# Carrying the later keys' sum through one row of the triangular operand, and rounding the attention weights on another engine

## The chip, the core and the metric

The kernel runs on one core of a Trainium2 chip. The metric is the device time of one execution in microseconds. A core has a matrix engine (TensorE, PE in the profile; its weight loads are PEld), a vector engine (VectorE, DVE), an engine for activation functions (ScalarE, ACT), a general engine (GpSimd, POOL) and one that only issues transfers (SyncE, SP). Each works through its own instructions in order; semaphores between them keep the order of the data. SBUF is the on-chip memory with 128 partitions, PSUM the smaller one that TensorE writes its sums to, here in banks of 128 x 512 fp32.

## What is computed

One layer of a decoder with 512 tokens and 1024 channels: a mixer of two branches (causal stick-breaking attention with 8 heads of 64, and a short gated convolution), a cross-attention into 256 memory tokens, a SwiGLU feed-forward part and a final norm. The change lies in the stick-breaking attention alone:

```python
z = jnp.einsum('bhqd,bhkd->bhqk', qb, kb) * scale
mask = k_pos < q_pos
log_fail = jnp.where(mask, jax.nn.log_sigmoid(-z), 0.0)
log_later = lax.cumsum(log_fail, axis=3, reverse=True) - log_fail
weights = jnp.where(mask, jnp.exp(jax.nn.log_sigmoid(z) + log_later), 0.0)
outs.append(jnp.einsum('bhqk,bhkd->bhqd', weights, vb))
```

With e = softplus(z), which is -log_sigmoid(-z), the weight of query t on key s is exp(z - sum of e over all keys from s up to t - 1). So each key needs the sum of `e` over itself and over all later keys.

## The kernel before

Scores are held transposed: keys on the partitions, queries along the columns. The heads are taken in four pairs `p`, and within a pair the key tiles of 128 from the last to the first, `kt` = 3, 2, 1, 0. Key tile `kt` sees the queries from its own first token on, so n = 512 - 128 kt columns for each head. For kt = 3 and 2 both heads of a pair share one PSUM bank (256 and 512 columns), for kt = 1 and 0 each head has its own (384 and 512); `heads_of` says which. This makes 16 steps, listed in `steps`.

All products are made in a rounded fp32 form (`F32R`) from a high and a low half: ScalarE casts the high half, VectorE subtracts it from the value to get the low half.

A step has three parts, each written by one function.

- `scores(p, kt)` (L399): TensorE makes z (L408). ScalarE makes |z|, exp(-|z|) and ln(1 + .) (L415 to L417), VectorE e = max(z, 0) + that (L418), GpSimd masks it (`causal`, L376), and `lsplit` (L388) makes the halves `l` (L390 on ScalarE, L391 on VectorE). For kt = 2 and 1 the running sum of all later tiles is then added to `e` (L430, VectorE), and that sum is split once more into the halves `r` (`rest`, L390 and L391). For kt = 3 the sum is `e` itself, so `l` serves.
- `weights(p, kt)` (L440): onto z in its bank TensorE adds, for kt < 3, minus the later tiles' sum (L448: `neg1`, all -1, by the two halves in `rest`) and then minus the sum within the tile (L451: `negtri`, the triangle of -1, by the two halves of `l`). ScalarE takes the exponential (L453) into `a`, GpSimd masks it, VectorE multiplies it by the token's norm factor `r0` and rounds it to `ah` (L457), and makes the low half `al` (L458).
- `values(p, kt)` (L463): TensorE multiplies both halves by the values (L470) into a bank that is summed over the key tiles. After kt = 0 the two parts of a head are joined (L478, L479).

The steps are spread over projections that have nothing to do with them (`project`: 24 matmuls of 512 columns, L154 to L156; their weights are loaded by SyncE, cast by ScalarE in L149 and split by VectorE in L150; `wpool` holds four of each, and their results leave their two PSUM banks through VectorE). In step i the loop writes the scores of step i + 1 into the middle of that step's projections, then the weights of step i, then the values of step i - 1. A planner, not the program, sets each engine's final order from these and its own estimates. The score banks are a ring of four (`pz`): a bank is free for new scores when its exponential is read. The tiles of `l` and `r` come from `lpool` and hold one step each of their kind.

Of the kernel before, what the change touches and what calls it, by code (L numbers as in the profile page):

```python
# [8 lines left out]
F32 = mybir.dt.float32  # L9
F32R = mybir.dt.float32r  # L10
AF = mybir.ActivationFunctionType
ALU = mybir.AluOpType

P = 128
# [3 lines left out]
TT = S // P  # L18
# [25 lines left out]
def hybrid_layer(ctx: ExitStack, tc: tile.TileContext, xT_d, memT_d, cols_d, wv_d, win_d,  # L44
# [18 lines left out]
    def nm(s):  # L63
        count[0] += 1
        return f"{s}{count[0]}"
# [7 lines left out]
    def f(ap):  # L73
        return ap.bitcast(F32)
# [19 lines left out]
                            pattern=[[-1, P]], channel_multiplier=1)  # L94
    negtri = cpool.tile([P, P], F32R, tag="negtri", name="negtri")
    nc.vector.tensor_copy(negtri, tri_f)
    eps_t = cpool.tile([P, 1], F32, tag="eps_t", name="eps_t")
    nc.vector.memset(eps_t, EPS)
    nc.vector.memset(neg_f, 1.0 / D)
# [271 lines left out]
    def span(kt):  # L371
        return kt * P, S - kt * P
# [6 lines left out]
    def heads_of(kt):  # L379

        return ((0, 1),) if kt >= TT - 2 else ((0,), (1,))

    def by_head(t, n):
        return t.rearrange("p (h c) -> p h c", c=n)

    rest, later = {}, {}

    def lsplit(t, n, tag, bufs):  # L388
        hi, lo = (lpool.tile([P, n], F32R, tag=tag, name=nm(tag), bufs=bufs) for _ in range(2))
        nc.scalar.copy(hi, t)  # L390
        nc.vector.tensor_tensor(out=lo, in0=t, in1=f(hi), op=ALU.subtract)  # L391
        return hi, lo

    def part_of(parts, hs, some, n):

        i = hs.index(some[0])
        return [t[:, i * n:(i + len(some)) * n] for t in parts]

    def scores(p, kt):  # L399
        c0, n = span(kt)  # L400
        keys = slice(kt * P, (kt + 1) * P)
        zs[p, kt] = []
        for hs in heads_of(kt):
            bank = ztile("z")
            zs[p, kt].append(bank)
            for i, h in enumerate(hs):
                for part in range(2):
                    nc.tensor.matmul(bank[:, i * n:(i + 1) * n], ks[p][h][:, keys],  # L408
                                     qs[p][h][part][:, c0:], start=i + part == 0, stop=part == 1,
                                     skip_group_check=True)  # L410
        for hs, bank in zip(heads_of(kt), zs[p, kt]):
            w = len(hs) * n
            z = bank[:, :w]
            e = tmp("e")[:, :w]
            nc.scalar.activation(e, z, AF.Abs)  # L415
            nc.scalar.activation(e, e, AF.Exp, scale=-1.0)
            nc.scalar.activation(e, e, AF.Ln, bias=1.0)  # L417
            nc.vector.scalar_tensor_tensor(out=e, in0=z, scalar=0.0, in1=e, op0=ALU.max,  # L418
                                           op1=ALU.add)
            causal(by_head(e, n))  # L420
            bufs = 4 // len(hs)
            sp[p, kt, hs] = lsplit(e, w, f"l{kt}", bufs)
            if kt == TT - 1:
                later[hs] = e
                rest[p, kt - 1, hs] = sp[p, kt, hs]
            elif kt > 0:
                t = by_head(e, n)[:, :, P:]
                before = heads_of(kt + 1)[0] if len(heads_of(kt + 1)) == 1 else hs
                old = by_head(part_of([later[before]], before, hs, n - P)[0], n - P)
                nc.vector.tensor_tensor(out=t, in0=t, in1=old, op=ALU.add)  # L430
                later[hs] = e
                rest[p, kt - 1, hs] = lsplit(e, w, f"r{kt}", bufs)

    def carried(p, kt, hs):

        n = span(kt + 1)[1]
        before = hs if (p, kt, hs) in rest else (0, 1)
        return [by_head(t, n) for t in part_of(rest[p, kt, before], before, hs, n)]

    def weights(p, kt):  # L440
        c0, n = span(kt)
        av[p, kt] = {}
        for hs, bank in zip(heads_of(kt), zs[p, kt]):
            w = len(hs) * n
            z = bank[:, :w]
            if kt < TT - 1:
                for part in carried(p, kt, hs):
                    nc.tensor.matmul(by_head(z, n)[:, :, P:], neg1, part, start=False, stop=False,  # L448
                                     skip_group_check=True)
            for part in sp[p, kt, hs]:  # L450
                nc.tensor.matmul(z, negtri, part, start=False, stop=True, skip_group_check=True)  # L451
            a = tmp("a")[:, :w]
            exps.append(nc.scalar.activation(a, z, AF.Exp))  # L453
            causal(by_head(a, n))
            ah, al = unit("ah")[:, :w], unit("al")[:, :w]
            r = r0[:, kt:kt + 1]
            nc.vector.tensor_scalar(out=ah, in0=a, scalar1=r, scalar2=None, op0=ALU.mult)  # L457
            nc.vector.scalar_tensor_tensor(out=al, in0=a, scalar=r, in1=f(ah), op0=ALU.mult,  # L458
                                           op1=ALU.subtract)
            for h in hs:  # L460
                av[p, kt][h] = part_of((ah, al), hs, (h,), n)
# [902 lines left out]
```

## Time and profile before

| what | us |
|---|---|
| median of 3 runs | 851.78 |
| lowest and highest | 851.10, 851.84 |
| the profiled execution | 850.78 |
| its span, first to last instruction | 849.1 |
| TensorE busy | 838.4 (99%) |
| VectorE busy | 656.2 (77%) |
| ScalarE busy | 458.4 (54%) |
| GpSimd busy | 159.7 (19%) |

The attention lies from about 44 to 196 us of the span. TensorE's clock was granted in full (0.998). A row of a group reads: line, engine, operation, output and inputs by the program's names, shape, count, then busy time in us and the mean of one in ns, then the engine's idle time just before them and what ended it. A row of the timeline reads: start, duration, engine, line, operation. A row of the chain of work that ended last has the start, the time that the piece held the chain, and the line with its count. A row of the waits says who waited for whom, then the total in us, how often, and the longest. "(+2 forms)" means that the group mixes several widths.

### The profile page before, as it was taken

To read this page: it belongs to the slowest core of one execution; us is meant where nothing else is said; L and a number is where in the kernel's file an instruction comes from. 1 tells how busy PE (TensorE), PEld (TensorE's weight loads), DVE (VectorE), ACT (ScalarE), POOL (GpSimd) and SP (SyncE) were. 2 spreads that over 40 slices of the span, in tenths; PEclk is the share of its full clock that TensorE was granted. 3 is DMA by queue.
4 is the path that set the end of the run, shared out by engine and by line. 5 is a ranking of instruction groups with operands and counts; after the bars stand their busy time and mean duration, and the time that the engine had idled before them with its cause. 6 is when DMAs were issued, how large, how long until landed. Compare 5 with 4: busy or idle time off the path is not lost.

```text
span 849.1 us, 12662 instructions
## 1 busy us (share of the span) xinstructions
PE 838.4 (99%) x4778; PEld 737.8 (87%) x4778; DVE 656.2 (77%) x1043; ACT 458.4 (54%) x810; POOL 159.7 (19%) x171
## 2 busy tenths in 40 slices
PE   9999999999999999999999999999999999999996
PEld 7888887888888899888888789999999999888885
DVE  7869989896766586587455679888887888999786
ACT  7567767474333344444444556655555555576664
POOL 0013221120566640163000101111111110000001
PEclk9999999999999999999999999999999999999999
DMA  8542232225588765566431335767767772465552
GB/s 298 156 142 64 93 117 75 75 76 183 200 310 309 297 245 190 174 230 247 151 81 49 112 75 142 181 174 187 186 176 187 190 186 85 155 221 196 171 187 99
DMA packets 50510, 141.62 MB, mean 167 GB/s; under 512 B 5521, under 2 KB 7569, under 8 KB 47634
## 3 DMA queue, kind: packets, MB, share of 16 engines
q1 hardware_dynamic: 40818, 105.93, 36.7%
q0 software_dynamic: 9344, 34.62, 15.7%
q8 instruction: 37, 0.61, 0.3%
q10 hardware_dynamic: 288, 0.28, 0.1%
q14 instruction: 23, 0.19, 0.1%
HBM read 125.07 MB, written 13.64 MB: 163 GB/s over the span
## 4 chain that ended last, share of the span: by engine, by line
PE 95%; DVE 3%; ACT 1%; issue 0%; DMA 0%; POOL 0%; SPq 0%; ACTq 0%
PE z L817 15%; PE p L1083 11%; PE y L817 7%; PE pr L154 7%; PE pr L155 7%; PE pr L156 7%; PE v L817 4%; PE r L156 3%; PE r L154 3%; PE r L155 3%; PE v L272 3%; PE mq L156 2%; PE mq L154 2%; PE br L155 2%; PE br L154 2%; PE mq L155 2%
## 5 line engine op out<-in xcount | busy, mean ns | idle before, releaser
L149 ACT CAST wh<-wr 128x1024 fp32r<-128x1024 f32 x84 | 88.0, 1052 | 151.7 <-issue 70.9
L150 DVE TENSOR_TENSOR wl<-wr,wh 128x1024 fp32r<-128x1024 f32 x84 | 110.6, 1318 | 37.0 <-ACT wh L149 36.9
L154 PE MATMUL pr<-xgh,wh 128*128 128x512 f32 x288 | 112.7, 391 | 0.0
L155 PE MATMUL pr<-xgl,wh 128*128 128x512 f32 x288 | 112.3, 390 | 0.0
L156 PE MATMUL pr<-xgh,wl 128*128 128x512 f32 x288 | 112.3, 390 | 0.0
L552 POOL TENSOR_TENSOR pre<-pre 128x512 f32<-128x512 f32 x44 | 72.1, 1642 | 31.4 <-DMA pre<-in_w_ffn_out_dram 29.1
L786 POOL DMA_DIRECT2D ws<-in_w_ffn_in_dram x22 | 26.5, 1207 | 258.4 <-DVE wf L807 104.7
L817 PE MATMUL z<-xdh,wf 128*128 128x256 f32 x352 | 70.5, 283 | 0.2 <-ACT sb L838 0.2
L156 PEld LDWEIGHTS pr<-xgh,wl 128*128 128x128 f32 x288 | 54.1, 188 | 11.5
L154 PEld LDWEIGHTS pr<-xgh,wh 128*128 128x128 f32 x288 | 54.1, 188 | 10.6
L155 PEld LDWEIGHTS pr<-xgl,wh 128*128 128x128 f32 x288 | 54.1, 188 | 10.3
L838 ACT COPY sa<-z 128x256 f32<-128x256 f32 x44 | 16.4, 373 | 79.2 <-PE z L817 79.1
L817 PEld LDWEIGHTS z<-xdh,wf 128*128 128x128 f32 x352 | 57.3, 189 | 0.5 <-ACT sb L838 0.4
L807 DVE TENSOR_TENSOR wf<-s,wf 128x512 fp32r<-128x512 f32 x44 | 30.3, 691 | 26.0 <-ACT wf L806 25.8
L817 PE MATMUL z<-xdl,wf 128*128 128x256 f32 x176 | 49.8, 283 | 0.0
L898 DVE TENSOR_TENSOR wl<-wr,wh 128x1024 fp32r<-128x1024 f32 x33 | 40.3, 1220 | 4.4 <-ACT wh L965 4.2
L965 ACT CAST wh<-wr 128x1024 fp32r<-128x1024 f32 x33 | 34.6, 1049 | 7.0 <-DMA wr<-sums 3.3
L817 PE MATMUL z<-xch,wf 128*128 128x256 f32 x176 | 35.4, 284 | 0.1
L817 PE MATMUL v<-xoh,wf 128*128 128x256 f32 x176 | 35.4, 283 | 0.0
L817 PE MATMUL y<-xch,wf 128*128 128x256 f32 x176 | 35.4, 283 | 0.0
L817 PE MATMUL z<-xf,wf 128*128 128x256 f32 x264 | 35.4, 283 | 0.0
L817 PE MATMUL y<-xoh,wf 128*128 128x256 f32 x176 | 35.3, 283 | 0.0
(337 smaller groups left out, 2403.3 us busy)
## 6 DMA issues: line engine op xcount, KB each, us to landing
wr<-in_w_in_dram SPq DMA_DIRECT2D x36, 512.0 KB, 3.3
pre<-in_w_ffn_out_dram POOLq DMA_DIRECT2D x11, 1024.0 KB, 8.0
sums<-pre POOLq DMA_DIRECT2D x11, 1024.0 KB, 5.0
ws<-in_w_ffn_in_dram SPq DMA_DIRECT2D x22, 512.0 KB, 3.7
wg<-in_w_ffn_in_dram SPq DMA_DIRECT2D x22, 512.0 KB, 4.0
ws<-in_w_ffn_in_dram POOLq DMA_DIRECT2D x22, 512.0 KB, 6.4
wr<-sums SPq DMA_DIRECT2D x22, 512.0 KB, 3.9
wr<-in_w_ffn_out_dram SPq DMA_DIRECT2D x16, 512.0 KB, 3.5
```

Of the source, the lines that this page charges most:

```text
L149: after(nc.scalar.copy(h2, raw), lead[-1:])
L150: lows.append(nc.vector.tensor_tensor(out=l2, in0=raw, in1=f(h2), op=ALU.subtract))
L154: nc.tensor.matmul(ps, a[0], b[0], start=start, stop=False, **kw)
L155: nc.tensor.matmul(ps, a[0], b[1], start=False, stop=False, **kw)
L156: nc.tensor.matmul(ps, a[1], b[0], start=False, stop=stop, **kw)
L552: nc.gpsimd.tensor_tensor(out=t[:, a, :], in0=t[:, a, :], in1=t[:, b, :], op=ALU.add)
L786: nc.gpsimd.dma_start(s13, a[:, 0:4:3, :], accum_op=ALU.add)
L807: nc.vector.tensor_tensor(out=w[:, 1, :], in0=raw, in1=f(w[:, 0, :]), op=ALU.subtract)
L817: nc.tensor.matmul(ps[:, :HS], a, b, start=i < 3 and k == 0 and j == 0, stop=k == KP - 1 and j == 2, skip_group_check=True)
L898: nc.vector.tensor_tensor(out=lo, in0=src, in1=f(hi), op=ALU.subtract)
L965: nc.scalar.copy(hi, raw)
L1083: nc.tensor.matmul(res[i][s2], a[:, ts], b, start=j == 0 and n == 0, stop=n == 2 and j == (BEHIND - 1 if (i, s2) == (5, 1) else NJ - 1))
```

## The change

The later tiles' sum no longer has matmuls of its own. It is written into the first key's row (partition 0) of the triangular operand `l` of the next tile: `negrow` is `negtri` with -1 in all of its first row, so whatever stands in the operand's row 0 is subtracted for every key of the tile. The first key's own `e`, which stood there, only concerns its own row of the result, and VectorE subtracts it from the bank's row 0 directly. `lsplit` puts both halves into one tile, and GpSimd clears row 0 for the tile's own first 128 queries, which see no later tile.

The sum itself is read off the bank: after the triangular matmul, row 0 of the bank holds the first key's z minus all `e` of this and of all later tiles. ScalarE keeps a copy of the raw row 0 (`before`, taken in `scores`), and in `weights` the new function `carry` subtracts the one from the other on VectorE, ScalarE casts the high half into row 0 of the next tile's operand, and VectorE makes the low half there. So the running sum in `e`, its second split and the `neg1` matmuls are gone, and each tile's triangular matmul now depends on the one before it.

Apart from that, `ah` is made by ScalarE (a copy with the scale `r0`) instead of VectorE.

```diff
+    negrow = lpool.tile([P, P], F32R, tag="negrow", name="negrow", bufs=1)
+    nc.vector.tensor_copy(negrow, tri_f)
+    nc.vector.tensor_copy(negrow[0:1, :], neg_f[0:1, :])
...
-    rest, later = {}, {}
-
-    def lsplit(t, n, tag, bufs):
-        hi, lo = (lpool.tile([P, n], F32R, tag=tag, name=nm(tag), bufs=bufs) for _ in range(2))
+    before = {}
+
+    def lsplit(t, n, heads, kt):
+
+        w = heads * n
+        both = lpool.tile([P, 2, w], F32R, tag=f"l{kt}", name=nm("l"), bufs=2 // heads)
+        hi, lo = both[:, 0, :], both[:, 1, :]
         nc.scalar.copy(hi, t)
         nc.vector.tensor_tensor(out=lo, in0=t, in1=f(hi), op=ALU.subtract)
+        if kt < TT - 1:
+            row = f(both)[0:1].rearrange("o a (h c) -> o a h c", c=n)
+            nc.gpsimd.memset(row[:, :, :, :P], 0.0)
         return hi, lo
...
             nc.scalar.activation(e, z, AF.Abs)
+            if kt > 0:
+                row = before[p, kt, hs] = lpool.tile([1, w], F32, tag="s", name=nm("s"), bufs=3,
+                                                     padded_shape=[1, 512])
+                nc.scalar.copy(row, z[0:1])
             nc.scalar.activation(e, e, AF.Exp, scale=-1.0)
...
             causal(by_head(e, n))
-            bufs = 4 // len(hs)
-            sp[p, kt, hs] = lsplit(e, w, f"l{kt}", bufs)
-            if kt == TT - 1:
-                later[hs] = e
-                rest[p, kt - 1, hs] = sp[p, kt, hs]
-            elif kt > 0:
-                t = by_head(e, n)[:, :, P:]
-                before = heads_of(kt + 1)[0] if len(heads_of(kt + 1)) == 1 else hs
-                old = by_head(part_of([later[before]], before, hs, n - P)[0], n - P)
-                nc.vector.tensor_tensor(out=t, in0=t, in1=old, op=ALU.add)
-                later[hs] = e
-                rest[p, kt - 1, hs] = lsplit(e, w, f"r{kt}", bufs)
...
+            if kt < TT - 1:
+                nc.vector.tensor_tensor(out=z[0:1], in0=z[0:1], in1=e[0:1], op=ALU.subtract)
+            sp[p, kt, hs] = lsplit(e, n, len(hs), kt)
+
+    def carry(p, kt, hs, z, n):
+
+
+        row = lpool.tile([1, len(hs) * n], F32, tag="c", name=nm("c"), bufs=2,
+                         padded_shape=[1, 512])
+        nc.vector.tensor_tensor(out=row, in0=before.pop((p, kt, hs)), in1=z[0:1], op=ALU.subtract)
+        for some in heads_of(kt - 1):
+            if hs[0] not in some and some[0] not in hs:
+                continue
+            src, = part_of([row], hs, some, n)
+            hi, lo = (by_head(t[0:1], n + P)[:, :, P:] for t in sp[p, kt - 1, some])
+            src = by_head(src, n)
+            nc.scalar.copy(hi, src)
+            nc.vector.tensor_tensor(out=lo, in0=src, in1=f(hi), op=ALU.subtract)
...
-            if kt < TT - 1:
-                for part in carried(p, kt, hs):
-                    nc.tensor.matmul(by_head(z, n)[:, :, P:], neg1, part, start=False, stop=False,
-                                     skip_group_check=True)
+            tri = negtri if kt == TT - 1 else negrow
             for part in sp[p, kt, hs]:
-                nc.tensor.matmul(z, negtri, part, start=False, stop=True, skip_group_check=True)
+                nc.tensor.matmul(z, tri, part, start=False, stop=True, skip_group_check=True)
             a = tmp("a")[:, :w]
             exps.append(nc.scalar.activation(a, z, AF.Exp))
+            if kt > 0:
+                carry(p, kt, hs, z, n)
             causal(by_head(a, n))
             ah, al = unit("ah")[:, :w], unit("al")[:, :w]
             r = r0[:, kt:kt + 1]
-            nc.vector.tensor_scalar(out=ah, in0=a, scalar1=r, scalar2=None, op0=ALU.mult)
+            nc.scalar.activation(ah, a, AF.Copy, scale=r)
```

More of the change, by code (lines that the diff above doesn't have):

```diff
@@ L420, in scores @@
             causal(by_head(e, n))
-            bufs = 4 // len(hs)
-            sp[p, kt, hs] = lsplit(e, w, f"l{kt}", bufs)
-            if kt == TT - 1:
-                later[hs] = e
-                rest[p, kt - 1, hs] = sp[p, kt, hs]
-            elif kt > 0:
-                t = by_head(e, n)[:, :, P:]
-                before = heads_of(kt + 1)[0] if len(heads_of(kt + 1)) == 1 else hs
-                old = by_head(part_of([later[before]], before, hs, n - P)[0], n - P)
-                nc.vector.tensor_tensor(out=t, in0=t, in1=old, op=ALU.add)
-                later[hs] = e
-                rest[p, kt - 1, hs] = lsplit(e, w, f"r{kt}", bufs)
[L434 to L438, printed above, removed]
+            if kt < TT - 1:
[13 more added lines that the diff above has]
+            nc.vector.tensor_tensor(out=lo, in0=src, in1=f(hi), op=ALU.subtract)
     def weights(p, kt):
```

## The prediction, made before the changed kernel was run

> **What bounds the kernel now.** I read the chain of work that ended last first, then the busy times of the stage that the change touches, then that stage's waits.
>
> ```profile
> PE 95%; DVE 3%; ACT 1%; issue 0%; DMA 0%; POOL 0%; SPq 0%; ACTq 0%
> 44.00:196.00 152.00, 151.04 (x720) 126.83 (x719) 130.81 (x213) 103.87 (x189) 35.37 (x60) 1.00 0.30 97
> ```
>
> The second row is the stage of the stick-breaking attention, from the first score matmul to the last value matmul. After the bounds and the length (152.00 us) come the busy times of PE, its weight loads, VectorE (DVE), ScalarE (ACT) and GpSimd (POOL). TensorE is without work for 0.96 us of it, so time leaves this stage only if TensorE gets less to do, and is lost wherever another engine makes it wait. VectorE stands at 130.81 of 152 (86%), ScalarE at 103.87 (68%): the first has little room, the second some.
>
> **Part 1: the matmuls that go.** The carry `neg1` x `rest` (L448) is no longer multiplied.
>
> ```profile
> L448 PE MATMUL z<-r,neg 128*128 128x384 f32 x16 | 4.1, 337 | 0.0
> L448 PE MATMUL z<-r,neg 128*128 128x256 f32 x16 | 3.2, 281 | 0.0
> L448 PE MATMUL z<-l,neg 128*128 128x256 f32 x8 | 1.6, 282 | 0.0
> 93.60 0.24 PE z L448 x2
> 114.13 0.35 PE z L448 x2
> ```
>
> The first three rows group them: 40 instructions, 24 with 256 columns and 16 with 384. Their mean durations include the pipeline, so the price is the pace in the chain: 0.24 us for a pair of 256 columns, 0.35 for a pair of 384. 12 x 0.24 + 8 x 0.35 = **5.7 us** that TensorE no longer streams. The stage's lower end for TensorE is 152.0 - 5.7 = 146.3 us. The triangular matmuls stay as many and as wide; `negrow` takes the place of `negtri` as their weights.
>
> **Part 2: VectorE.** In each of the four head pairs the changed groups are: kt=3 one of 256 columns, kt=2 one of 512, kt=1 two of 384, kt=0 two of 512.
>
> ```profile
> L430 DVE TENSOR_TENSOR e<-e,e 128x256 f32<-128x256 f32 x12 | 5.7, 486 | 0.0
> L391 DVE TENSOR_TENSOR r<-e,r 128x384 fp32r<-128x384 f32 (+1 forms) x12 | 7.4, 617 | 0.8 <-ACT r L390 0.8
> L457 DVE TENSOR_SCALAR ah<-a,r 128x512 fp32r<-128x512 f32 (+2 forms) x24 | 11.1, 464 | 3.8 <-POOL a L376 3.8
> L418 DVE SCALAR_TENSOR_TENSOR e<-z,e 128x512 f32<-128x512 f32 x12 | 8.0, 684 | 1.8 <-ACT e L417 1.8
> L391 DVE TENSOR_TENSOR l<-e,l 128x384 fp32r<-128x384 f32 x8 | 4.4, 554 | 0.8 <-ACT l L390 0.8
> L391 DVE TENSOR_TENSOR l<-e,l 128x256 fp32r<-128x256 f32 x4 | 1.7, 424 | 2.0 <-ACT l L390 2.0
> L313 DVE TENSOR_TENSOR k<-qk,k 64x512 fp32r<-64x512 f32 x8 | 5.5, 686 | 0.3
> ```
>
> The first three rows go: 5.7 + 7.4 + 11.1 = 24.2 us. What comes works on one partition. The last row shows that 64 partitions cost what 128 do (686 against 684 ns for 512 columns), so I price one partition like 128. No row shows one partition on VectorE, nor VectorE writing the score bank in PSUM: it could be nearly free, or dearer by about as much as the difference between the rows above. New are the subtraction of `e`'s row from the bank (12 of 512, 8 of 384 columns), the difference row (4 of 512, 8 of 384, 4 of 256) and the low half of the carry (8 of 384, 12 of 256): 16 x 0.684 + 16 x 0.554 + 4 x 0.424 + 8 x 0.554 + 12 x 0.424 = 31.0 us. **Net +6.8 us**: VectorE comes to 137.6 us against 146.3 us for TensorE, 94%.
>
> [...]
>
> **Part 3: ScalarE.**
>
> ```profile
> L390 ACT CAST l<-e 128x512 fp32r<-128x512 f32 x12 | 7.5, 621 | 11.5 <-POOL e L376 11.5
> L390 ACT CAST l<-e 128x384 fp32r<-128x384 f32 x8 | 4.0, 517 | 1.6 <-POOL e L376 1.6
> L390 ACT CAST l<-e 128x256 fp32r<-128x256 f32 x4 | 1.6, 406 | 8.8 <-POOL e L376 8.8
> L390 ACT CAST r<-e 128x384 fp32r<-128x384 f32 (+1 forms) x12 | 6.5, 548 | 5.9 <-DVE e L430 5.8
> L176 ACT ACTIVATE vmh<-vm,rm 128x512 fp32r<-128x512 f32 x4 | 2.7, 690 | 1.9 <-PE vm L156 1.9
> L201 ACT COPY vrow<-varb 1x512 f32<-1x512 f32 x1 | 0.6, 576 | 1.8 <-PE varb L190 1.8
> ```
>
> The `r` casts go (6.5 us). The last row is a copy of one partition out of PSUM: 576 ns, so one partition is hardly cheaper here. Coming: the score rows (4 of 512, 8 of 384, 4 of 256: 8.2 us), the high halves of the carry (8 of 384, 12 of 256: 9.0), and `ah` with its scale, 0.07 us dearer than a cast by the `vmh` row (12 x 0.69 + 8 x 0.59 + 4 x 0.48 = 14.9). **Net +25.6 us**: 129.5 us, 88% of 146.3.
>
> **Part 4: GpSimd, the start, the memory.** 20 memsets of a row are new.
>
> ```profile
> 4.46 0.43 DVE L241 CAST wvh<-wk 128x512 fp32r<-128x512 f32 x1 [2.08 <-DMA wk<-in_w_value_dram]
> L347 POOL MEMSET cu<- x4: 100/102/104, 0.9 to 108.2; 128x2 f32 x4
> 0.79 0.20 POOL masks.py:197 MEMSET ident<- 128x128 f32 x1 [0.29 <-POOLq L1354]
> 99.08 1.61 POOL L498 TENSOR_TENSOR accm<-accm,mk 128x256 f32<-128x256 f32 x2
> 99.14 0.95 DVE L457 TENSOR_SCALAR ah<-a,r 128x512 fp32r<-128x512 f32 x1 [0.30 <-POOL a L376]
> ```
>
> From 0.10 us for 2 elements and 0.20 for 128 I estimate 0.3 us for 256 and 0.5 for 512 (16 and 4 of them): 6.8 us on an engine that is busy for 35 of 152. They cost time only where the triangular matmul waits for one (0.3 us, used below). The 99.08 and 99.14 rows show an `ah` stretched to 0.95 us beside a GpSimd add, against 0.46 on the mean of its kind: half of the time beside it. At that rate the memsets would stretch VectorE by 3.4 us. I take 0, since a memset reads nothing, and keep 3.4 for the range.
>
> [...]
>
> Two casts of 128 columns for `negrow` stand at the start, where VectorE waits 2.08 us for the first weights anyway (first row): nothing. The loads and their queues are not touched.
>
> **Part 5: where TensorE now waits.** Two places, both behind VectorE's queue.
>
> ```profile
> 102.49 1.22 DVE L150 TENSOR_TENSOR wl<-wr,wh 128x1024 fp32r<-128x1024 f32 x1
> 109.86 1.22 DVE L150 TENSOR_TENSOR wl<-wr,wh 128x1024 fp32r<-128x1024 f32 x1
> 110.78 0.56 PE L408 MATMUL z<-q,k 128*128 128x128 f32 x4
> 112.38 0.68 DVE L391 TENSOR_TENSOR l<-e,l 128x512 fp32r<-128x512 f32 x1
> 115.29 0.46 PE z L451 x2
> 149.51 0.68 DVE L391 TENSOR_TENSOR l<-e,l 128x512 fp32r<-128x512 f32 x1
> 153.23 0.46 PE z L451 x2
> 187.00 0.69 DVE L391 TENSOR_TENSOR l<-e,l 128x512 fp32r<-128x512 f32 x1 [0.47 <-ACT l L390]
> 189.43 0.46 PE z L451 x2
> ```
>
> First, a score bank is now free only when VectorE has read its row, not when ScalarE's exponential is done. The scores at 110.78 need the bank of kt=1. TensorE comes there 0.72 us sooner (three pairs of 0.24), at 110.06. If the row read stands behind the `wl` of 109.86, it ends at 111.08 + 0.55 = 111.6: a wait of 1.5 us, with the next projection queued behind it. If it stands ahead: 0. I take the middle, 0.75, at the three such places (pair to pair): 2.3 us.
>
> Second, the triangular matmul of kt=0 is where a pair has most of its new VectorE work ahead of it: between the kt=2 and the kt=0 matmuls 6.2 us come (two subtractions each at kt=1 and kt=0, rows for kt=2 and kt=1, four low halves) and 2.7 go (two `e` sums, two `r` halves, one `ah`), net 3.5. Three `wl` of 1.22 us stand there (first and last quoted), each for a projection three ahead (`wpool` holds four), so they can slide; if two do, 3.5 - 2.4 + 0.3 for the memset = 1.4 us is added. Today's margins from the end of the last `l` to its matmul are 2.2, 3.0 and 1.7 us in the pairs 1 to 3 (I take none for pair 0); TensorE comes 1.42 us sooner (three pairs of 0.24, two of 0.35). That leaves waits of 0.6, 0 and 1.1 us. The first is already paid by the 0.75 ahead of it; the last stands. Sum of both: 2.3 + 1.1 = **3.4 us**.
>
> **The sum.** -5.7 + 3.4 = -2.3 us. The profiled execution took 850.78 us (span 849.1 and 1.7 around it), 1.0 below the median of the runs, 851.78. Against the median: **849.5 us**. The ends of the unknowns: no new wait, 846.1; with 1.5 at all three places and no `wl` slid (3.8 added, waits of 3.0, 2.2 and 3.5 at kt=0), 10.2 us of waits, 856.3.
>
> **The rivals.** *Full gain.* The planner orders VectorE so that the row reads and carries go first; TensorE waits nowhere: 846.1 us. For it stands this row of the windows:
>
> ```profile
> 100.00:111.00 11.00, 11.00 (x56) 9.38 (x54) 10.89 (x17) 7.44 (x13) 2.15 (x5) 1.00 0.31 98
> ```
>
> From 100 to 111 us VectorE is busy for 10.89 of 11.00 us today and TensorE still doesn't wait. Against it: three engines at 88% or more.
>
> *VectorE becomes the bound.*
>
> ```profile
> DVE e L418 <- ACT e L417: 5.1, 3, 3.0
> DVE ah L457 <- POOL a L376: 3.8, 7, 1.7
> DVE l L391 <- ACT l L390: 3.3, 6, 1.0
> ACT l L390 <- POOL e L376: 21.8, 13, 4.2
> ACT r L390 <- DVE e L430: 5.8, 5, 1.9
> ```
>
> If VectorE's own waits of 12.2 us (first three rows) stay as they are, `al` waiting for ScalarE instead of `ah` for GpSimd, it needs 137.6 + 12.2 = 149.8 us; with an additional 1 to 2 us for 20 carries that wait for ScalarE's cast, about 151.3: 851.1 us, the same as now. Against it: some of those waits only show that VectorE had caught up.
>
> *ScalarE, in order, becomes the bound, and the kernel is slower.* Its waits for GpSimd and VectorE (27.6 us in the last two rows) are round trips inside the chain of one group. With 129.5 us of work it would need 157.1 us if none of them were filled; from less than 5.1 us filled (18%) it is longer than today's 152. Its weight casts then come late, and every projection with them. At a tenth filled, 154.3: **854.1 us**; none filled, and the row reads on top, about 858. For it: `ah` and the carry add 24 + 20 more casts that wait for another engine, so the waits may well grow. Against it: today's waits are the gaps into which the planner can put new work.
>
> **How the numbers follow.** Partial gain as summed: 0.28. Full gain: 0.15. VectorE the bound, no change: 0.25. ScalarE the bound, slower: 0.32. Below 0.2% (1.7 us) a measurement of this kernel can't be told from no change. Faster takes the first two and nothing of the others: 0.43; same 0.25; slower 0.32. The range runs from just under the full gain to near the end of the slower case: 845.8 to 857.0 us.
>
> **What would show it.** Right: no L448 left, TensorE's waits in the stage grown from 1 us to 3 or 4, behind the bank's row read and behind the kt=0 carry; VectorE near 138 us and ScalarE near 129 in it. Wrong: one-partition instructions clearly cheaper than 0.4 us (full gain); ScalarE idle behind VectorE's difference row or GpSimd's mask while `wh` casts are queued (slower); TensorE idle ahead of projections for `wl` (VectorE or ScalarE the bound).

## The result, and the profile after

The changed kernel takes 855.24 us (median of 5 runs, 854.36 to 855.82) against 851.78 of the kernel before (851.10 to 852.09): ratio 1.0041, with an interval of 1.0026 to 1.0056. It is slower by 3.5 us, where 849.5 was forecast; the time lies inside the range. Its profiled execution took 854.89 us.

The chain of work that ended last, by engine, on the page of the changed kernel:

```profile
PE 83%; DVE 6%; ACT 6%; POOL 2%; DMA 1%; issue 1%; SPq 0%; POOLq 0%; ACTq 0%
```

The windows of the same kernel give the stage of the attention, which now ends at 200.6 us instead of 196.6 (columns as in the prediction, then clock and DMA):

```profile
44.00:200.60 156.60, 151.18 (x686) 121.10 (x684) 137.18 (x222) 122.58 (x236) 42.45 (x80) 1.00 0.27 88
```

TensorE's share of the chain fell from 95% to 83%: VectorE and ScalarE now end stretches of it. TensorE is without work for 5.4 us of the stage (0.96 before), at a full clock. Of the 9 to 10 us of new waits that are counted below, the other 5 us or so sit inside records that look busy (151.18 us in all for 151.04 before, although 5.7 us of matmuls went): matmuls that no longer overlap their neighbours. Without a wait, matmuls of 512 columns start 0.23 us apart and their records last 0.39 (60.00 to 61.13 us of the changed kernel), so by these records a start that comes up to 0.16 us late leaves no idle time. The waits show better on the weight loads: these also wait for the operand that the matmul multiplies by the weights, in the changed kernel 2.4 us for `ah`, where the weight is `v` (row of L482 below). First the kernel before, then the changed one, groups of weight loads in the stage; the number behind the second bar is the idle time just before them:

```profile
L408 PEld LDWEIGHTS z<-q,k 128*128 128x128 f32 x63 | 10.4, 189 | 2.5 <-ACT a L453 1.1
L451 PEld LDWEIGHTS z<-l,negtri 128*128 128x128 f32 x48 | 8.3, 189 | 0.4
L470 PEld LDWEIGHTS o<-al,v 128*128 128x128 f32 x32 | 6.0, 188 | 1.8 <-DVE al L458 1.3
L470 PEld LDWEIGHTS o<-ah,v 128*128 128x128 f32 x32 | 6.0, 188 | 0.6
L448 PEld LDWEIGHTS z<-r,neg 128*128 128x128 f32 x32 | 6.0, 189 | 1.0
L448 PEld LDWEIGHTS z<-l,neg 128*128 128x128 f32 x8 | 1.5, 190 | 0.3
```

```profile
L417 PEld LDWEIGHTS z<-q,k 128*128 128x128 f32 x64 | 10.4, 188 | 4.8 <-DVE c L443 3.2 <-issue 0.3
L461 PEld LDWEIGHTS z<-l,negrow 128*128 128x128 f32 x40 | 7.5, 188 | 5.3 <-issue 2.0 <-DVE l L451 2.0
L482 PEld LDWEIGHTS o<-al,v 128*128 128x128 f32 x32 | 6.0, 189 | 2.7 <-DVE al L470 2.2
L482 PEld LDWEIGHTS o<-ah,v 128*128 128x128 f32 x32 | 6.0, 188 | 3.2 <-ACT ah L469 2.4 <-DVE ot L491 0.2
L461 PEld LDWEIGHTS z<-l,negtri 128*128 128x128 f32 x8 | 1.5, 189 | 0.6 <-DVE l L397 0.3
```

Read in groups: waits ahead of the scores grew by 2.3 us (4.8 - 2.5), ahead of the triangular matmuls by 5.5 (5.3 + 0.6 - 0.4), ahead of the values by 3.5 (2.7 + 3.2 - 1.8 - 0.6); those of the matmuls that went, 1.3, are gone. Together 10.0 us. Of the triangular matmuls' 5.3 us only 2.0 name VectorE's low half of the carry; another 2.0 stand as "issue", for which the profile shows no releaser. The length of the stage says nearly the same. Its last value matmul, in the kernel before and in the changed one:

```profile
196.59 0.39 PE L470 MATMUL o<-al,v 128*128 128x512 f32 x1
```

```profile
200.63 0.50 PE L482 MATMUL o<-al,v 128*128 128x512 f32 x1
```

Its first score matmul starts at 43.98 before and at 44.84 after. From there to the last value matmul it is 152.6 us before and 155.8 after, although 5.7 us were taken out, so 8.9 us of waits came. (The later beginning is not read as an effect of the change: in the runs below the stage begins anywhere from 43.6 to 44.8 us.)

One place shows how they arise. Timeline of the changed kernel (start, duration; in brackets the wait and its releaser):

```profile
103.69 1.07 PE L417 MATMUL z<-q,k 128*128 128x512 f32 x4
107.49 1.14 ACT L430 ACTIVATE e<-e 128x512 f32<-128x512 f32 x2
107.85 1.20 DVE L153 TENSOR_TENSOR wl<-wr,wh 128x1024 fp32r<-128x1024 f32 x1
109.38 1.21 DVE L153 TENSOR_TENSOR wl<-wr,wh 128x1024 fp32r<-128x1024 f32 x1
110.04 0.87 PE L461 MATMUL z<-l,negrow 128*128 128x384 f32 x4
111.18 1.21 DVE L153 TENSOR_TENSOR wl<-wr,wh 128x1024 fp32r<-128x1024 f32 x1
112.98 1.27 DVE L431 SCALAR_TENSOR_TENSOR e<-z,e 128x512 f32<-128x512 f32 x2
114.05 1.21 ACT L396 CAST l<-e 128x512 fp32r<-128x512 f32 x2 [2.99 <-POOL e L379]
115.17 0.86 ACT L463 ACTIVATE a<-z 128x384 f32<-128x384 f32 x2
117.17 0.53 DVE L443 TENSOR_TENSOR c<-s,z 1x384 f32<-1x384 f32 x1
117.76 0.67 PE L417 MATMUL z<-q,k 128*128 128x128 f32 x4 [1.14 <-DVE c L443]
```

The scores of kt=0 are there at 104.8 and ScalarE is done with them at 108.6, but VectorE makes `e` from them only at 112.98: three weight splits `wl` and the convolution's instructions stand ahead. ScalarE then waits 2.99 us with its casts of `l`, and its exponential of kt=1, whose triangular matmul ended at 110.9, stands behind these casts. VectorE's difference row, the new release of that bank, comes at 117.17, and TensorE waits. The windows of this stretch, the changed kernel and the one before:

```profile
100.00:120.00 20.00, 18.56 (x87) 14.95 (x86) 19.75 (x32) 14.25 (x27) 6.14 (x13) 1.00 0.28 94
```

```profile
100.00:120.00 20.00, 20.00 (x100) 17.12 (x99) 18.04 (x28) 12.72 (x24) 4.88 (x9) 1.00 0.28 93
```

VectorE is busy for 19.75 of 20 us; TensorE loses 1.44 us.

### The profile page after: what moved, and what is told of

It reads as the page before. It is cut to its first block, busy times and chain, and to the rows that moved or that the text cites. A ratio compares the mean times of both kernels' runs of the same rounds, so it can differ in the third digit from the quotient of the medians.

```text
span 853.2 us, 12672 instructions
## 1 busy us (share of the span) xinstructions
PE 837.7 (98%) x4738; PEld 731.1 (86%) x4738; DVE 661.9 (78%) x1053; ACT 477.2 (56%) x858; POOL 166.3 (19%) x191
## 4 chain that ended last, share of the span: by engine, by line
PE 83%; DVE 6%; ACT 6%; POOL 2%; DMA 1%; issue 1%; SPq 0%; POOLq 0%; ACTq 0%
PE z L829 15%; PE p L1095 11%; PE y L829 7%; PE pr L158 5%; PE pr L157 4%; PE pr L159 4%; PE v L829 4%; PE r L158 3%; PE r L157 3%; PE r L159 3%; PE v L275 2%; PE mq L159 2%; PE mq L157 2%; PE mq L158 2%; PE br L159 2%; PE br L158 2%
```

## The experiments

Every kernel was timed beside the kernel before. Ratios are to that, with their intervals; the changed kernel stands at 1.0041 (1.0026 to 1.0056). The kernel before ran at 851.5 to 852.1 us beside them, so a difference between two medians of this table is good to about half a microsecond.

| label | median us | ratio | interval |
|---|---|---|---|
| e1_ah_back | 867.33 | 1.0187 | 1.0167 to 1.0206 |
| e2_ah_only | 850.77 | 0.9990 | 0.9981 to 0.9999 |
| e3_no_l448 | 846.43 | 0.9942 | 0.9925 to 0.9959 |
| e4_no_carry | 849.01 | 0.9969 | 0.9956 to 0.9982 |
| e5_carry_first | 853.94 | 1.0024 | 1.0014 to 1.0033 |
| e6_row_copy | 856.04 | 1.0049 | 1.0034 to 1.0064 |
| e7_wl_lag | 873.71 | 1.0254 | 1.0237 to 1.0271 |
| e8_mem_moved | 854.60 | 1.0031 | 1.0019 to 1.0043 |
| e9_dummy | 854.94 | 1.0040 | 1.0025 to 1.0055 |
| e10_narrow | 851.65 | 1.0001 | 0.9992 to 1.0010 |
| e11_no_carry_sub | 843.80 | 0.9907 | 0.9891 to 0.9924 |
| e12_first_mem | 856.34 | 1.0058 | 1.0043 to 1.0073 |
| e13_no_memset | 854.32 | 1.0031 | 1.0019 to 1.0043 |
| e14_no_sub | 852.29 | 1.0007 | 0.9997 to 1.0016 |
| e15_narrow_sub | 853.87 | 1.0023 | 1.0014 to 1.0032 |
| e16_lo_pool | 860.45 | 1.0104 | 1.0089 to 1.0119 |
| e17_no_bank | 855.78 | 1.0052 | 1.0035 to 1.0069 |
| e18_narrow_no_bank | 850.77 | 0.9991 | 0.9982 to 1.0000 |

### The parts one by one

The saving alone, in the kernel before:

```diff
-            if kt < TT - 1:
-                for part in carried(p, kt, hs):
-                    nc.tensor.matmul(by_head(z, n)[:, :, P:], neg1, part, start=False, stop=False,
-                                     skip_group_check=True)
```

> The kernel before without the 40 carry matmuls (the later tiles' sum is left out of the weights); all the work of the other engines stays. Both theories: TensorE saves the 5.7 us of the prediction and waits no more than before, 846.1. If it stays above 849, the other engines already bound the stage before the change and the saving was never there to be had.

5.0 us less (0.0058 of 851.5): the saving is real and of about the size of Part 1. Windows of this kernel:

```profile
44.00:196.00 152.00, 150.32 (x700) 124.75 (x699) 136.20 (x219) 107.69 (x193) 34.90 (x60) 1.00 0.33 107
```

VectorE is busy for 136.20 of 152 here, more than in the changed kernel (134.43 of the same stretch), and TensorE hardly waits. The stage itself ends at 192.1 here, and VectorE works for 132.7 of its 148.1 us, 90%, where the changed kernel has 88%. So a VectorE as full as this does not cost by itself; TensorE has to need what stands in its queue, and soon. Here the later sums are still made, but no matmul waits for them.

`ah` alone, once moved in the kernel before, once moved back in the changed one:

```diff
-            nc.vector.tensor_scalar(out=ah, in0=a, scalar1=r, scalar2=None, op0=ALU.mult)
+            nc.scalar.activation(ah, a, AF.Copy, scale=r)
```

> The kernel before with only one part of the change: ah on ScalarE; the carry matmuls stay. Theory V: ScalarE has room and VectorE loses 11.1 us, so nothing is late and TensorE bounds it as before: 851.0 to 852. Theory S: the waits of ScalarE for GpSimd's mask delay the weight casts and the values' operands: 854 or more.

> The changed kernel with the high half of the weights (ah) made on VectorE again, as before the change. Theory V (VectorE's queue is too long, so the difference row and the carry come late and TensorE waits for them): VectorE gets 11.1 us more in a stage in which it already works 137 us, so it is slower than the changed kernel's 855.2, about 858 to 862. Theory S (ScalarE, in order, stands still for ah until GpSimd has masked the weights, 12.1 us in the trace of the changed kernel, and everything behind it is late): those waits go, about 848 to 851.

On ScalarE it costs nothing (0.9990), although ScalarE takes on 14.7 us of work. Back on VectorE the changed kernel loses 12 us more, past the 858 to 862 that were expected. Windows of e2_ah_only (103.87 us of ScalarE in the kernel before):

```profile
44.00:196.00 152.00, 151.56 (x724) 127.49 (x723) 122.58 (x190) 118.55 (x213) 33.53 (x60) 1.00 0.31 98
```

Most of e1's loss is one event. Its timeline, then windows of the same kernel:

```profile
103.60 10.59 POOL L510 TENSOR_TENSOR accm<-accm,mk 128x256 f32<-128x256 f32 x2 [0.22 <-ACT mk L505]
114.13 0.30 POOL L400 MEMSET l<- 1x256 f32 x1
114.48 0.69 PE L461 MATMUL z<-l,negrow 128*128 128x384 f32 x1 [8.72 <-POOL l L400]
```

```profile
103.60:114.20 10.60, 2.16 (x9) 1.31 (x7) 10.60 (x16) 4.94 (x10) 10.52 (x3) 0.78 0.40 117
110.00:114.00 4.00, 0.00 (x0) 0.00 (x0) 4.00 (x6) 0.00 (x0) 4.00 (x1) 0.50 0.89 280
```

The 0.3 us memset of row 0 is behind two GpSimd adds that took 10.59 us while VectorE was busy without a gap, and the triangular matmul waits 8.72 us for it. The clock granted to TensorE falls to 0.50 meanwhile and is full again only at about 119.9 us, an estimated 2.7 us more (last section). These 11.4 us are most of the 14.2 by which this profiled execution (869.07) is longer than the changed kernel's. So e1 overstates what 11 us of VectorE work cost by themselves.

The carry taken out of the changed kernel, then in a second kernel the subtraction in the bank and the memsets as well:

```diff
-                row = before[p, kt, hs] = lpool.tile([1, w], F32, tag="s", name=nm("s"), bufs=3,
-                                                     padded_shape=[1, 512])
-                nc.scalar.copy(row, z[0:1])
...
-                carry(p, kt, hs, z, n)
```

> The changed kernel without the copies of the raw rows, the difference rows and the carried halves (the later tiles' sum is left out); the subtraction in the bank, the memsets and ah on ScalarE stay. VectorE loses 18.4 us, ScalarE 16, and no triangular matmul depends on the one before it. Theory V: TensorE's waits all but go: 846 to 848. Theory S: the waits for ah stay, about 4 us of TensorE's time: 850 or more.

```diff
-                nc.vector.tensor_tensor(out=z[0:1], in0=z[0:1], in1=e[0:1], op=ALU.subtract)
...
-            nc.gpsimd.memset(row[:, :, :, :P], 0.0)
```

> The kernel without a carry (849.0) with the subtraction in the bank and the memsets left out as well; first keys' e is then counted for every key. VectorE loses another 12.5 us, GpSimd 7. If these two make the rest of the loss against the 846.4 that the saved matmuls alone give: 846 to 847. If it stays near 849, the rest lies with ah on ScalarE.

Without the carry 849.0, between the two expectations and 6.2 us below the changed kernel; without the other two as well 843.8, another 5.2 and below the 846 to 847 expected. Windows of e11_no_carry_sub:

```profile
44.00:196.00 152.00, 152.00 (x714) 127.91 (x713) 116.61 (x171) 115.06 (x205) 29.88 (x60) 1.00 0.34 108
```

TensorE has no idle time at all. The stage runs from 44.75 to 189.68, 144.9 us, where the kernel before, less the 5.7 us of Part 1, would have 146.9. So the lower end is real and lies some 2 us below that of Part 1 (843.8 for 846.1): the kernel before had waits of that size itself, more than its 0.96 us of idle time show.

### Order, priority and the slide of `wl`

The carry given priority in the planner; GpSimd's sums of squares moved to other steps; and both:

```diff
-                carry(p, kt, hs, z, n)
+                with tc.high_priority():
+                    carry(p, kt, hs, z, n)
```

> The changed kernel with the carry (difference row, its cast and its low half) given priority in the planner's order over the work written before it; the same instructions. Theory Q (the order in VectorE's queue: the row read and the carry stand behind work that isn't urgent): the waits for the score bank (5.1 us in the trace of the changed kernel) and for the carry's low half (about 3) shrink by half or more: 850 to 852.5. Theory L (plain load and round trips between the engines, whatever the order): within 1 us of 855.2.

```diff
-MEM_AT = (1, 3, 5, 7)
+MEM_AT = (1, 4, 5, 8)
```

> The changed kernel with two of the four memory-square steps moved by one step, away from kt=0, so that GpSimd's long adds don't stand ahead of the mask of kt=0's weights. Theory G (GpSimd in order: in the changed kernel 4.2 us of adds hold back the masks at the end of pair 0, and TensorE waits some 2 us for the halves of the weights): 852 to 853.5. Theories Q and L: within 1 us of 855.2.

> The changed kernel with both orders that helped a little: the carry with priority, and the memory squares moved. Complete in what it computes. If the two gains add (1.3 and 0.6 us): 853.3. Below 851.5 it would be a version better than the kernel before; I expect it to stay above.

Each alone gains about 1 us (853.9, short of the 850 to 852.5 hoped for, and 854.6), both together lose 1 (856.3, for 853.3 expected). The gains don't add: differences of about 1 us are what a changed order alone makes here, and are not read as a cause below.

The assumption of Part 5 that weight splits slide behind the attention, forced (each split held until the max-and-add instructions that were written before the preceding split are done):

```diff
+        after(lows[-1], soft[1][-2:])
+        soft[1] = list(soft[0])
...
-            nc.vector.scalar_tensor_tensor(out=e, in0=z, scalar=0.0, in1=e, op0=ALU.max,
-                                           op1=ALU.add)
+            soft[0].append(nc.vector.scalar_tensor_tensor(out=e, in0=z, scalar=0.0, in1=e,
+                                                          op0=ALU.max, op1=ALU.add))
```

> The changed kernel with VectorE's weight splits (wl) held behind the max-and-add of the scores written before them, except the first split after each; so two of the three that stand ahead of kt=0's scores slide, as the prediction assumed. Theory Q: the kt=0 matmuls and the row reads come up to 2.4 us sooner in each pair: 850 to 853. Theory L: 855 or slower.

873.7 us, 18 more than the changed kernel. Waits in this kernel (total, times, longest), then windows of it:

```profile
PEld o L484 <- ACT ah L471: 7.4, 4, 3.8
PEld pr L161 <- DVE wl L153: 3.8, 3, 1.9
```

```profile
78.00:82.00 4.00, 3.65 (x12) 3.36 (x13) 4.00 (x8) 1.55 (x3) 1.50 (x1) 0.50 0.00 0
```

TensorE now waits for `wl` itself and longer for `ah`, and runs at half its clock in this window (0.50). In this form the splits have no room to slide; a gentler order was not tried, so it isn't shown that none exists.

### Which of the new waits: the bank, the chain, the memset

Three dependences cut, one at a time. First the bank freed by a copy of its row on ScalarE, so that VectorE reads SBUF:

```diff
-        nc.vector.tensor_tensor(out=row, in0=before.pop((p, kt, hs)), in1=z[0:1], op=ALU.subtract)
+        nc.scalar.copy(row, z[0:1])
+        nc.vector.tensor_tensor(out=row, in0=before.pop((p, kt, hs)), in1=row, op=ALU.subtract)
```

> The changed kernel with the bank's row copied to SBUF by ScalarE, so that VectorE's subtraction no longer holds the score bank; 16 copies (about 8 us) more on ScalarE, and one more handoff in the carry. Theory Q in the form that the bank is what counts: the 5.1 us of waits for it go and 2 come back by the longer carry: about 852. If the carry's own way counts: 855 to 858.

The same with no read of the bank at all, at the same length:

```diff
+        raw = before.pop((p, kt, hs))
+        nc.vector.tensor_tensor(out=row, in0=raw, in1=raw, op=ALU.subtract)
```

> The changed kernel with the difference row made from the raw row twice, in SBUF, instead of from the bank (the later tiles' sum is left out). Load and count of the instructions stay; the bank is free when the exponential has read it, as before the change, and the row no longer waits for the triangular matmul. If the hold on the bank is a cause of its own: 851 to 852.5. If the load finds another place to make TensorE wait: 854 to 855.5.

The chain from tile to tile cut, at the same load: the halves go into a tile that is already used.

```diff
-            hi, lo = (by_head(t[0:1], n + P)[:, :, P:] for t in sp[p, kt - 1, some])
+            hi, lo = (by_head(t[0:1], n) for t in part_of(sp[p, kt, hs], hs, some, n))
```

> The changed kernel with all its instructions, but the two halves of the carry are written into row 0 of the tile just used instead of the next one (the later tiles' sum is left out of the weights). The load on VectorE and ScalarE and the hold on the score bank stay; only the way from one triangular matmul to the next is cut. Theory C (that chain, tile to tile, is what TensorE waits for): close to the 849.0 without any carry, 849 to 851. Theory L (the work of the carry in VectorE's and ScalarE's queues, wherever it is written): 854 to 855.5.

And the memsets left out (the two lines of `lsplit`):

> The changed kernel without GpSimd's memsets (row 0 keeps the first key's own e for the tile's own queries). GpSimd loses 6.9 us, and the triangular matmul no longer waits for it. If the memset, as the last step ahead of that matmul, is what counts: 851 to 853. If it is VectorE's load: within 1 us of 855.2.

856.0, 855.8, 854.9, 854.3: no single dependence is worth more than 1 us. In e6 the scores' wait falls from 3.2 to 0.8 us, but that of the weight loads for `ah` grows from 2.4 to 5.3. The largest wait of e17_no_bank shows how that comes:

```profile
PEld z L417 <- ACT a L464: 4.4, 2, 2.4
```

Freed from the row read (3.2 us in the changed kernel), the scores wait even longer for ScalarE's exponential, which is late for the reason of the timeline above.

### How much: the size of VectorE's new work

The carry's instructions shortened to 32 columns a head, on VectorE and on ScalarE (its row copies and high halves), number and dependences kept; the same without the bank's row; the subtraction in the bank left out; the same shortened:

```diff
-                nc.scalar.copy(row, z[0:1])
+                nc.scalar.copy(by_head(row, n)[:, :, :32], by_head(z[0:1], n)[:, :, :32])
...
-            hi, lo = (by_head(t[0:1], n + P)[:, :, P:] for t in sp[p, kt - 1, some])
-            src = by_head(src, n)
+            hi, lo = (by_head(t[0:1], n + P)[:, :, P:P + 32] for t in sp[p, kt - 1, some])
+            src = by_head(src, n)[:, :, :32]
```

> The changed kernel with the row copies, the difference rows and both halves of the carry made for 32 columns of each head only (the rest of the later tiles' sum is left out). Every dependency and every instruction stays; VectorE loses some 11 us of the carry's 18, ScalarE some 7. Theory C: the chain is only a little shorter, 853 to 855. Theory L: most of the 6.2 us between the changed kernel and the one without a carry go, 849.5 to 851.5.

> e10 (the carry made for 32 columns only, 851.7) with the difference row made from SBUF as in e17. If the hold on the bank makes the 2.6 us that are left between e10 and the kernel without a carry (849.0): 848.5 to 849.5. If the count of instructions makes them: 851 to 852.

```diff
-                nc.vector.tensor_tensor(out=z[0:1], in0=z[0:1], in1=e[0:1], op=ALU.subtract)
```

> The changed kernel without the subtraction of the first key's e in the score bank (that key then lacks its own e). VectorE loses 12.5 us, the carry and the memsets stay. If VectorE's load in the stage is what counts, 137.2 - 12.5 = 124.7 us, less than the 130.8 of before: 848 to 850.

```diff
-                nc.vector.tensor_tensor(out=z[0:1], in0=z[0:1], in1=e[0:1], op=ALU.subtract)
+                nc.vector.tensor_tensor(out=z[0:1, :32], in0=z[0:1, :32], in1=e[0:1, :32],
+                                        op=ALU.subtract)
```

> The changed kernel with that subtraction made for the first 32 columns only (the rest of the first key's row lacks its own e). The instruction and all its waits stay, VectorE loses some 8.5 us. If load counts: two thirds of what e14 gains. If the place counts (between the mask and the matmul): within 1 us of 855.2.

Here the time moves: 851.65 (-3.6 against the changed kernel), 850.8, 852.3 (-3.0) and 853.9 (-1.4). Only the last two change VectorE's work alone. e18 falls between its two expectations, e14 stays above the 848 to 850 expected, and of its 3.0 us only 1.4 come with the length of the instruction (e15), little more than a changed order makes. Windows of e14_no_sub; VectorE is busy for 8 us less than in the same 152 us of the changed kernel (134.43):

```profile
44.00:196.00 152.00, 146.85 (x674) 120.96 (x673) 126.33 (x200) 122.29 (x234) 38.93 (x80) 0.99 0.29 92
```

TensorE's largest waits stay where they were. The row of e15_narrow_sub:

```profile
PEld z L417 <- DVE c L444: 8.2, 5, 4.0
```

The wait named is longer than in the changed kernel (3.2 us) and the kernel is faster: a wait that is named shows where TensorE stood, not how much is lost in all.

At last the carry's low half taken from VectorE to GpSimd:

```diff
-            nc.vector.tensor_tensor(out=lo, in0=src, in1=f(hi), op=ALU.subtract)
+            nc.gpsimd.tensor_tensor(out=lo, in0=src, in1=f(hi), op=ALU.subtract)
```

> The changed kernel with the low half of the carry made by GpSimd instead of VectorE; the same result. VectorE loses 9.8 us; GpSimd gets 20 subtractions of one row, by its adds of 256 columns about 0.7 to 1.1 us each, ahead of its masks. If VectorE's load decides and GpSimd has room (42 of 157 us busy): 851 to 853. If GpSimd's queue becomes the next one to wait for: 855 or more.

860.45. Its groups on GpSimd:

```profile
L451 POOL TENSOR_TENSOR l<-c,l 1x384 fp32r<-1x384 f32 x8 | 13.6, 1709 | 3.9 <-ACT l L450 3.9
L451 POOL TENSOR_TENSOR l<-c,l 1x256 fp32r<-1x256 f32 x12 | 12.7, 1063 | 5.8 <-ACT l L450 5.8
PEld z L461 <- POOL l L451: 7.9, 9, 1.6
```

Two to three times VectorE's duration (below), in the middle of the chain. The last row is a wait: the triangular matmuls now stand 7.9 us for these low halves, for 2.0 in the changed kernel. Less load on VectorE, longer latency, and the kernel is slower; how much of it is GpSimd's own queue was not isolated.

Of all these only e2_ah_only (850.8) keeps the whole computation and is not slower than the kernel before, and it is level with it.

## Why the prediction was wrong

Groups of the changed kernel against which the Parts are read:

```profile
L435 DVE TENSOR_TENSOR z<-z,e 1x512 f32<-1x512 f32 x12 | 8.2, 683 | 1.7 <-POOL e L379 1.6
L451 DVE TENSOR_TENSOR l<-c,l 1x384 fp32r<-1x384 f32 x8 | 4.4, 550 | 0.0
L451 DVE TENSOR_TENSOR l<-c,l 1x256 fp32r<-1x256 f32 x12 | 5.4, 452 | 0.4 <-ACT l L450 0.4
L400 POOL MEMSET l<- 1x256 f32 x16 | 4.8, 302 | 11.5 <-DVE l L397 11.5
```

**Part 1** (5.7 us of matmuls) held: e3_no_l448 gains 5.0, and e11_no_carry_sub shows that the lower end can be reached.

**Part 2** held: one partition costs what 128 do (683 ns for 684 assumed, 550 for 554), and writing to the bank is no dearer (the 683 ns are of the subtraction that does it). VectorE stands at 137.18 us for 137.6; over the whole execution it grew by 5.7 us (661.9 for 656.2) where 6.8 were summed. For `ah` itself VectorE's instruction is the shorter one (535 ns before, 716 on ScalarE after, for 512 columns), but the runs don't speak against the move: nothing is lost by it in e2_ah_only (850.77 us), and e1_ah_back (867.33) is slower, though mostly by one event.

**Part 3** was a little high in the stage, 122.58 us for 129.5, though not by its new instructions: `ah`, the high halves and the score rows sum to 31.3 us by their groups, for 32.1. Over the whole execution the durations of its instructions sum to 23.6 us more than before, but it is busy for only 18.8 more (477.2 for 458.4): the records of neighbouring instructions overlap, which a sum of mean durations doesn't see. **Part 4** held in size (302 ns for 0.3 us); the memsets cost 0.9 us in e13_no_memset, within what order alone does. But in e1 a memset delayed by its own engine's queue became the longest wait, 8.72 us, where Part 5 had priced a memset ahead of a triangular matmul at 0.3.

**Part 5 failed**: the new waits were put at 3.4 us and are about 9 (855.2 less the 846.1 of the full gain; 8.9 by the length of the stage). The step that failed is the first sentence, that TensorE now waits in two places. Sorted by place, the waits of the changed kernel's weight loads that have a row of their own are:

| place | in the sum, us | measured, us |
|---|---|---|
| scores of the next pair, for the bank's row read | 2.3 | 1.9 |
| triangular matmuls of kt=0 | 1.1 | 2.0 |
| scores of kt=0, for the bank's row read | none | 1.6 |
| triangular matmuls of kt=1, 2 and 3 | none | 2.3 |
| the values' operands, beyond those of before | none | 3.5 |

At its own two places the sum is nearly right, 3.9 us for 3.4, but partly by luck: three waits of 0.75 were put at the bank, and there are one of 1.56 (at 117.76 in the timeline) and one of 0.29 for which the profile shows no releaser. (All rows sum to 11.3 us; 1.1 of the scores' waits were there before.) That the waits ahead of all scores grew by 2.3 us, the very number of that term, is luck too. The larger part is the other 7.4 us, at places that Part 5 put at nothing without a reason.

The sentence that two of three `wl` slide behind did not hold either. In the pair of the timeline none of the three slid (107.85, 109.38, 111.18). The pairs 2 and 3 had only two `wl` in that place in the kernel before, not three, and one of the two slid in each. With the slide as it was, the prediction's own sum would be 0.75 + 3.0 + 1.0 + 2.3 = 7.1 us and 853.2: slower than before, the right way, but for waits of 6.3 us at the matmuls of kt=0 where 2.0 are measured. Forcing the splits back costs 18 us (e7_wl_lag), which doesn't show what a free slide would give.

Why these places wait is shown in part. Each had been thought of with a margin of its own, but cutting a place moves the wait (e6, e9, e17), while taking the new work out shortens the kernel (e10, e14, e15, e4, e11; in e10, e4 and e11 ScalarE's part goes with VectorE's). The subtraction is one such piece: it stands ahead of the low half of `l`, and everything behind it, the difference row, `al`, the next `e`, comes later by its length, then ScalarE's casts and exponentials that wait for these. Not all of it is VectorE's queue: 2.7 us of the waits for the values stand at 87 to 90 us, behind `ah`, which waits for GpSimd's masks, and these stand behind two adds that took 4.17 us together (last section). Moving these adds gains 0.6 us (e8_mem_moved), no more than order does.

**The rivals.** "ScalarE in order" had the sign and nearly the time (854.1), but not for its reason. Waits of ScalarE in the changed kernel:

```profile
ACT ah L469 <- POOL a L379: 12.1, 11, 3.5
ACT l L396 <- POOL e L379: 4.9, 5, 3.0
ACT l L450 <- DVE c L443: 2.0, 2, 1.2
```

These are 19.0 us, where the two waits of before were 27.6: the total fell by a third, and 122.6 + 19.0 = 141.6 us is well within the 156.6 of the stage. No weight load of a projection waits for a late weight cast, and e2_ah_only, which gives ScalarE the same `ah`, isn't slower. ScalarE's order does take part, though: in the timeline the exponential of kt=1 stands behind casts that wait 2.99 us for `e`. "VectorE becomes the bound" named the engine whose queue is in most of the waits, and its price, a stage of 151.3 us, was too low: it counted 12.2 us of VectorE's own waits, but its idle time in the stage was 152.00 - 130.81 = 21.2 us before and is 156.60 - 137.18 = 19.4 after. "Full gain" fell: the measured time is 9 us above it, and e5_carry_first, where the difference rows of the timeline come at 110.86 instead of 117.17, gains 1.3 us.

**Open.** Load alone doesn't decide: e3 runs at 846.4 with 136 us on VectorE, e10 and e14 at about 852 with 126 in the same stretch. What separates them is that TensorE needs the new short instructions, each one a handover between engines; that this is the reason was not isolated. Of the 6.2 us of the carry 3.6 go with its length on VectorE and ScalarE together (e10), 0.9 more with the bank's hold (e18), and the last 1.8 (e18 to e4) with the instructions as such; of those no run tells latency, queue place and number apart, and the last two figures are near what order alone does.

## What to carry to other kernels

Work taken off a saturated TensorE only pays if the engines that take it over can deliver in time: here 5.7 us of matmuls went, about 9 us of waits came, and the kernel is 3.5 us slower. How full such an engine is doesn't tell: the kernel before has VectorE busy for 10.89 of 11.00 us from 100 to 111 us, and TensorE doesn't wait. Look at what stands in its queue between producer and consumer and at the slack there today. Price a new step in a dependent chain as a delay of all that stands behind it in its queue, at every place where TensorE needs something from there, and don't assume that unrelated work slides out of its way unless the order in the trace shows that it can. If cutting one named wait only makes another appear, take work out of the queue that they share.

## What the hardware showed besides

**TensorE's long wait in e1_ah_back costs twice.** Rows of this kernel after the 8.72 us of waiting:

```profile
117.85 0.63 PE L158 MATMUL pr<-xgl,wh 128*128 128x512 f32 x1
118.28 0.63 PE L159 MATMUL pr<-xgh,wl 128*128 128x512 f32 x1
120.40 0.39 PE L159 MATMUL pr<-xgh,wl 128*128 128x512 f32 x1
120.63 0.39 PE L157 MATMUL pr<-xgh,wh 128*128 128x512 f32 x1
```

Starts are 0.43 us apart in the first two and 0.23 in the last two. From 114.5 to about 119.9 us TensorE ran at half its clock (0.50 on the mean of 114 to 118 us), an estimated 2.7 us lost on top: half of these 5.4 us. The order of the event: the last matmul ended at 105.8 us, and the clock fell at about 109.6 (an estimate from its mean of 0.95 over 106 to 110 us), 3.8 us later; work began again at 114.5, and the clock returned 5.4 us after that (its mean over 118 to 122 us is 0.77, and from 119.94 on the records last 0.40 us or less instead of 0.63). How long a wait has to be for this was not isolated. In the changed kernel's stage no wait of a weight load passes 1.6 us, and the clock stayed at 1.00.

**GpSimd's adds can be stretched many times over.** In the changed kernel:

```profile
82.18 4.17 POOL L510 TENSOR_TENSOR accm<-accm,mk 128x256 f32<-128x256 f32 x2
103.69 1.75 POOL L510 TENSOR_TENSOR accm<-accm,mk 128x256 f32<-128x256 f32 x2 [0.53 <-ACT mk L505]
```

Two adds of the same shape took 1.75 us, 4.17, and 10.59 in e1_ah_back. VectorE was busy for 1.57 us beside the first, 2.75 beside the second and all the time beside the last, 90%, 66% and 100%, so its load alone doesn't explain it. VectorE is stretched too: in the kernel before, a sum of 256 columns (L430 at 100.02) took 0.95 us beside such an add, where the median of its kind is 0.42. What decides was not isolated, and the legend of the profile calls GpSimd's spans rough.

**Short is not cheap.** In e15_narrow_sub a subtraction of 32 columns takes 184 ns:

```profile
L435 DVE TENSOR_TENSOR z<-z,e 1x32 f32<-1x32 f32 x20 | 3.7, 184 | 3.9 <-POOL e L379 3.6
```

A sixteenth of the 512 columns costs more than a quarter of their 683 ns.
